# A hybrid decoder layer on one core: the sampled tokens' gate and norm by themselves, values turned through memory, a later residual, another order at the start, the last quarter in parts

## The chip, the cores and the metric

The kernel runs on one core of a Trainium2 chip. A core has TensorE (matrix products and transposes, its results in PSUM), VectorE, ScalarE and GpSimd (elementwise work, sums, activations), SyncE, which here only issues DMA transfers, and DMA engines between device memory and SBUF, the on-chip memory of 128 partitions. Each engine works through its own queue in order and waits on semaphores. The metric is the device time in microseconds, the median of several runs; one further run is profiled.

## The reference

One layer of a decoder for two groups: one new sequence of 1024 tokens ("prompt") and eight sequences with one token each and a carried state ("sample"). Model width 1024, all arrays float32.

```python
proj = rmsnorm(x, norm1_w) @ w_in            # 1024 -> q, f, i, g (1024 each), z (1024), xBC (1536), dt (16)
# group A, HGRN2: 8 heads of 128
f = lb + (1 - lb) * sigmoid(f_r); k = 1 - f; q = silu(q_r); v = i_r
S = f * S + k v^T;  o_a = rmsnorm(q S) * silu(g_r)          # a scan over the tokens
# group B, Mamba-2: 16 heads of 64, 2 groups, state 128
xBC = silu(conv4(xBC)); dt = softplus(dt_r + bias)
S = exp(A dt) S + dt x B^T;  y = S C + D x                  # a scan over the tokens
y = rmsnorm(y * silu(z), per group of 512)
x = x + concat(o_a, y) @ w_out
gate, val = split(rmsnorm(x, norm2_w) @ w_up)               # 2 x 2816
x = x + (silu(conv3(gate)) * val) @ w_down
y = rmsnorm(x, final_norm_w)
```

Both states and the convolutions' last rows are returned too.

## The kernel before, in words

Activations lie with features on partitions and the 1032 tokens (1024 of the prompt, then 8 sampled) along the free axis. Every large product is made of three passes on rounded operands (`fp32r`): high part by high part, low by high, high by low. So each weight tile is loaded (`ws`), rounded on ScalarE (`wh`, L190) and subtracted on VectorE (`wl`, L192); `wload` (from L180) does this with two buffers.

TensorE's order is written by hand. A list of jobs, one for each block of 128 output features of the input projection (three chunks of 344 tokens, 72 matmuls) or two blocks of the output projection, is the main stream. Side streams (the two SSD groups, the eight HGRN heads) are Python generators, and `drive` advances the main stream by a number of matmuls for each weight that a generator yields. `after(n, work)` calls a piece of work n main matmuls later; `spread` does so piece by piece. The other engines' queues are ordered by the framework's scheduler, which follows the order of the program only loosely; `fetch` (L172) keeps a load behind the weight load issued last.

The stages in order of time:

- Start: `first_norm` (L106) norms three tiles of tokens a chunk: squares and root on ScalarE, reciprocal and scaling on VectorE (`xn`, L118), transposes (`tp`), rounding into `hh` and `hl` (L125, L126). Two projection blocks (x8, x10) are interleaved. Their two weight tiles are loaded and rounded before the norms in the program.
- Jobs x0 to x3; then x9, x11, x4 to x7 beside SSD group 0; z0 to z3, f0, q0, v0 beside SSD group 1; sg0 and z4 to z7 alone. `ssm_decode(g, i)` (L625) is the SSD step of the eight sampled tokens for one block: loads of B, C and state, scaling on ScalarE, products on VectorE (L639, L640), GpSimd (L642) and a reduction (L643). It is called as x5, x7, z0, z1 and z4 to z7 begin, and its result goes into the last 8 columns of the block `Xg[g][i]`. `ssm_gate(g)` multiplies all 1032 columns by silu(z) (L671), sums the squares, and `rstd` makes the norm with a product by `ones` (`ms`) and `rstd_of` (L646 to 651). `tail` (L690) scales the four blocks (L694) and stores them to `mix_d`.
- Heads 0 to 7: `head(h)` (from L829) runs beside the jobs f, q, v, sg of head h+1, the last one beside o8.0 to o12.2. It begins with the transposes of `v`: one of the sampled tokens' (`vd`, L834) and eight of 128 by 128 (`vtp`, L839), which ScalarE copies to `vt` (L840). `vt` is first read by `kv` (L958) and then by `o`. Then come seven levels of a tree of products (`a`), with scalings on VectorE (L872, L873), and the storage of `v` is overwritten from the first of them (L901).
- Output projection: rows 8 to 15 of `mix_d` (jobs o8.m, o12.m, each two blocks of features), then rows 0 to 7 in two halves of tokens. `residual_load` and `residual` add the layer's input: `token_blocks` (L770) rearranges it in device memory by 32-token blocks (`xb_d`), VectorE transposes 32 by 32 blocks (L793), and GpSimd adds (L790). This is done in the o8 jobs, whose sums ScalarE copies from PSUM (L1064); the o12 jobs add on VectorE (L1066). The sampled tokens' input is transposed by TensorE for each block (`xtd`, L797), into a PSUM bank of which there is one (`nx`).
- The MLP's up projection (`ua`, `ub`), the down projection (`dn`), whose last four row blocks run quarter by quarter of the tokens in the order 3, 0, 1, 2. After each quarter 128 tokens at a time are transposed back (`fin`, L1461), squared (L1463), rooted, scaled and stored.

Of the kernel before, what the change touches and what calls it, by code (L numbers as in the profile page):

```python
# [16 lines left out]
P = 128  # L17
DM = 1024
# [32 lines left out]
def hybrid_layer(  # L51
# [54 lines left out]
    def first_norm(tiles):  # L106
        xs = []
        for i in tiles:
            xt, t0, n = xtm[i]
            xn = [half("xn"), half("xn")]  # L110
            ss = keep.tile([P, 4], F32, tag="ss", bufs=4, name=nm("ss"))
# [3 lines left out]
            A.activation(ss[:n, 3:4], ss[:n, 2:3], AF.Sqrt, bias=epsc[:n], scale=1.0 / DM)  # L115
            V.reciprocal(ss[:n, 3:4], ss[:n, 3:4])
            for i in range(2):
                V.tensor_scalar(xn[i][:n], xt[:n, i * 512:(i + 1) * 512], ss[:n, 3:4], None, op0=ALU.mult)  # L118
            xs.append((xn, t0, n))
        c0, c1 = xs[0][1], xs[-1][1] + xs[-1][2]  # L120
        for k in range(KT):
            tp = bank("tp")
            for xn, t0, n in xs:
                PE.transpose(tp[:, t0 - c0:t0 - c0 + n], xn[k // 4][:n, (k % 4) * P:(k % 4 + 1) * P], ident[:n, :n])
            A.activation(hT_hi[k][:, c0:c1], tp[:, :c1 - c0], AF.Copy, scale=col("n1", k))  # L125
            V.scalar_tensor_tensor(hT_lo[k][:, c0:c1], tp[:, :c1 - c0], col("n1", k),  # L126
                                   hT_hi[k][:, c0:c1].bitcast(F32), op0=ALU.mult, op1=ALU.subtract)
# [52 lines left out]
    def wload(src, kt, m=P, kept=None):  # L180
# [9 lines left out]
        A.copy(wh[:, :n], ws[:, :n])  # L190
        if not again:
            V.tensor_tensor(wl[:, :n], ws[:, :n], wh[:, :n].bitcast(F32), op=ALU.subtract)  # L192
        if kept is not None:
            if again:
                SP.dma_start(wl.bitcast(F32), wl_d[kept[0]])
            else:
                SP.dma_start(wl_d[kept[0]], wl.bitcast(F32))
# [164 lines left out]

    def xbc_close(j, ext):
# [6 lines left out]
        A.activation(acc[:, T:NT], acc[:, T + 3:T + 32:4], AF.Silu)  # L370
        return acc

    def xbc_job(j, put):
        ext = []
        def begin():
            ext.append(xbc_open())
            if j in (5, 7):
                ssm_decode(0, (5, 7).index(j))
# [13 lines left out]
    first = [(j, wload(w_in_[0, :, OFF_X + j * P:OFF_X + (j + 1) * P], KT), xbc_open()) for j in (8, 10)]  # L392
    for i in range(3, 9):
        load_x(i)
    vec_cols(0)
    for c in range(NCH):
        first_norm(range(3 * c, 3 * c + 3))
# [28 lines left out]
    G.memset(dtr[:, :NT], 0.0)  # L426
# [98 lines left out]
    for g in range(4):  # L525
        rows = slice(32 * g, 32 * g + 32)
        V.tensor_copy(mlow[rows], lowf[rows, :, rows])
        V.tensor_copy(eyec[rows], ident[rows, rows])
# [96 lines left out]
    def ssm_decode(g, i):  # L625
        j = g * 4 + i
        xdd = small.tile([P, 2, ND], F32, tag="xdd", name=nm("xdd"))
        xdec = Xg[g][i][:, T:NT]
# [15 lines left out]
        V.scalar_tensor_tensor(xdec, xdec, d_bc[:, j:j + 1], xdd[:, 1, :], op0=ALU.mult, op1=ALU.add)  # L644

# [7 lines left out]
    def ssm_gate(g):  # L653
        acc = []

        def z_job(i):
            j = g * 4 + i

            def begin():
                if i == 0:  # L660
                    acc.append(tl("g", "gacc"))
                if g:
                    ssm_decode(1, i)
                elif i < 2:
                    ssm_decode(0, i + 2)

            def evict(c, cs, ps):
                Y = Xg[g][i][:, cs]
                sz = tl("z", "sz")[:, :CH]
                A.activation(sz, ps, AF.Silu)  # L670
                V.tensor_tensor(Y, Y, sz, op=ALU.mult)  # L671
# [5 lines left out]
                if i == 3:  # L677
                    after(36 + 14 * g, lambda: rstd(c))
            in_job(f"z{j}", OFF_Z + j * P, evict, begin=begin)

        def rstd(c):
            cs = chunks[c]
            ps = bank("ms", "nx")
            mm(ps[:, :CH], ones, acc[0][:, cs])
            rstd_of(acc[0][:, cs], tl("z", "nt")[:, :CH], ps[:, :CH], 512)
# [4 lines left out]
        def tail():  # L690
            for i in range(4):
                j = g * 4 + i
                Y = Xg[g][i][:, :NT]
                V.scalar_tensor_tensor(Y, Y, col("sn", j), acc[0][:, :NT], op0=ALU.mult, op1=ALU.mult)  # L694
                SP.dma_start(mix_d[8 + j], Y)

# [54 lines left out]
    vd_d = dram.tile([H, ND, P], F32, name="vd_d")  # L751
    hr_d = dram.tile([H, 4, 256], F32, name="hr_d")

    am = const.tile([P, NC, P], F32, name="am")
    G.memset(am, 0.0)
# [3 lines left out]
    V.tensor_tensor(selod, ident[:, 0:ND], ident[:, 32:32 + ND], op=ALU.add)  # L759
# [9 lines left out]

# [736 lines left out]
```

## Time and profile before

| What | us |
|---|---|
| Median of 3 runs | 1764.88 (1764.72 to 1768.95) |
| The profiled execution's own time | 1763.89 |
| Its span, first to last instruction | 1762.2 |
| TensorE busy in it | 1713.2 (97%) |
| VectorE busy | 1105.4 (63%) |
| ScalarE busy | 812.3 (46%) |
| GpSimd busy | 482.0 (27%) |

A row of a group of instructions has line, engine, operation, output and inputs, shape and count, then busy us, mean ns of one, and the engine's idle time just before them with what ended it. A row of a timeline has start and length in us. A row of waits has engine, operation and line, what it waited for, then the sum in us, the times, and the longest. Matmuls overlap one another, so that the time from one's start to the next one's start is shorter than the length that is shown.

### The profile page before, as it was taken

The page shows a single profiled execution, that of the slowest core. Times are in us where ns is not written, and L with a number is a line of the kernel's source. Part 1 is how long each engine was busy: PE and PEld are TensorE (multiplying, and loading weights), DVE is VectorE, ACT ScalarE, POOL GpSimd, SP SyncE. Part 2 cuts the span into 40 slices and gives each one's busy share as a digit, 9 for nine tenths or more (in the row PEclk, how much of TensorE's full clock was granted, in tenths as well). Part 3 has the DMA queues.
Part 4 walks back from the last instruction along what each step waited for, and adds up shares of the span by engine and source line. Part 5 has one row for each costly group of instructions (what it writes and reads, how often), then busy time and mean ns, then how long its engine had stood idle before and what let it go on. Part 6 is the DMA issues. An engine that isn't in the chain of part 4 may idle for free. (4 is left out here: it accounts for less than half of the span.)

```text
span 1762.2 us, 38558 instructions
## 1 busy us (share of the span) xinstructions
PE 1713.2 (97%) x16111; PEld 1662.8 (94%) x16111; DVE 1105.4 (63%) x1988; ACT 812.3 (46%) x1450; POOL 482.0 (27%) x485
## 2 busy tenths in 40 slices
PE   7999899999999999999899999999999999999998
PEld 6999799998999999999799989999999999999997
DVE  6668966575554554466636688776667777445545
ACT  7577698454544454454423374334333434111114
POOL 2103332120110110112220355666666664000002
PEclk9999999999999999999899999999999999999999
DMA  5355744643321332234336742222222226422312
GB/s 166 68 147 155 189 117 136 179 139 105 88 89 51 98 87 80 69 115 143 110 113 212 245 127 73 73 85 85 85 73 73 80 78 217 152 85 78 98 61 97
DMA packets 249828, 199.17 MB, mean 113 GB/s; under 512 B 47212, under 2 KB 220822, under 8 KB 249638
## 3 DMA queue, kind: packets, MB, share of 16 engines
q1 hardware_dynamic: 249366, 196.61, 36.8%
q8 instruction: 126, 2.06, 0.5%
q14 instruction: 48, 0.39, 0.1%
q0 software_dynamic: 288, 0.10, 0.0%
HBM read 154.11 MB, written 46.94 MB: 114 GB/s over the span
## 5 line engine op out<-in xcount | busy, mean ns | idle before, releaser
L93 PE MATMUL mm<-hh,wh 128*128 128x344 f32 x1248 | 405.9, 326 | 2.0 <-issue 1.2
L93 PE MATMUL mm<-hl,wh 128*128 128x344 f32 x1248 | 405.5, 325 | 0.0
L93 PE MATMUL mm<-hh,wl 128*128 128x344 f32 x1248 | 402.4, 323 | 0.0
L93 PEld LDWEIGHTS mm<-hh,wh 128*128 128x128 f32 x1248 | 235.4, 189 | 6.5 <-issue 3.9
L93 PEld LDWEIGHTS mm<-hl,wh 128*128 128x128 f32 x1248 | 235.4, 189 | 4.5 <-issue 3.3
L93 PEld LDWEIGHTS mm<-hh,wl 128*128 128x128 f32 x1248 | 235.7, 189 | 1.8 <-issue 1.4
L190 ACT CAST wh<-ws 128x1024 fp32r<-128x1024 f32 x96 | 100.6, 1047 | 254.1 <-PE dn L93 135.0
L93 PE MATMUL ub<-uh,wh 128*128 128x258 f32 x704 | 199.3, 283 | 3.1 <-DVE fext L1319 2.7
L93 PE MATMUL ub<-ul,wh 128*128 128x258 f32 x704 | 199.0, 283 | 0.0
L93 PE MATMUL ub<-uh,wl 128*128 128x258 f32 x704 | 198.7, 282 | 0.0
L93 PE MATMUL dn<-ah,wh 128*128 128x256 f32 (+1 forms) x640 | 181.1, 283 | 2.0 <-DVE x L1436 2.0
L93 PE MATMUL dn<-al,wh 128*128 128x256 f32 (+1 forms) x640 | 180.6, 282 | 0.0
L93 PE MATMUL dn<-ah,wl 128*128 128x256 f32 (+1 forms) x640 | 180.1, 281 | 0.0
L192 DVE TENSOR_TENSOR wl<-ws,wh 128x1024 fp32r<-128x1024 f32 x88 | 108.7, 1235 | 75.7 <-ACT wh L190 68.6
L93 PE MATMUL mm<-mh,wh 128*128 128x258 f32 x512 | 148.2, 289 | 4.1 <-ACT x L1064 2.8
L93 PE MATMUL ua<-uh,wh 128*128 128x258 f32 x528 | 149.6, 283 | 1.3 <-DVE val L1331 1.3
L93 PE MATMUL ua<-ul,wh 128*128 128x258 f32 x528 | 149.3, 283 | 0.0
L93 PE MATMUL ua<-uh,wl 128*128 128x258 f32 x528 | 148.4, 281 | 0.0
L93 PE MATMUL mm<-ml,wh 128*128 128x258 f32 x512 | 146.9, 287 | 0.8 <-DVE ml L1024 0.8
L93 PE MATMUL mm<-mh,wl 128*128 128x258 f32 x512 | 146.5, 286 | 0.0
L93 PEld LDWEIGHTS ub<-uh,wh 128*128 128x128 f32 x704 | 132.9, 189 | 3.8 <-DVE fext L1319 2.9
L1269 DVE TENSOR_TENSOR wl<-wt,wh 128x512 fp32r<-128x512 f32 x88 | 89.6, 1037 | 74.2 <-ACT wh L1268 73.9
(351 smaller groups left out, 4037.2 us busy)
## 6 DMA issues: line engine op xcount, KB each, us to landing
ws<-in_w_in_dram SPq DMA_DIRECT2D x52, 512.0 KB
ws<-in_w_up_dram SPq DMA_DIRECT2D x44, 512.0 KB
ws<-in_w_out_dram SPq DMA_DIRECT2D x24, 512.0 KB
act_d<-val SPq DMA_DIRECT2D x22, 516.0 KB
al<-act_d SPq DMA_DIRECT2D x22, 516.0 KB
ws<-in_w_down_dram SPq DMA_DIRECT2D x22, 512.0 KB
ml<-mix_d SPq DMA_DIRECT2D x48, 172.0 KB
csb<-cs_d SPq DMA_DIRECT2D x32, 256.0 KB
```

Source lines behind the costliest of these rows:

```text
L93: PE.matmul(out, lhsT, rhs, start=start, stop=stop)
L190: A.copy(wh[:, :n], ws[:, :n])
L192: V.tensor_tensor(wl[:, :n], ws[:, :n], wh[:, :n].bitcast(F32), op=ALU.subtract)
L1269: V.tensor_tensor(lo[:, cs], sums[name], hi[:, cs].bitcast(F32), op=ALU.subtract)
```

## The change

Five parts, shown cut to their core.

**Sampled tokens apart.** `ssm_decode` works in a tile of its own (`xdk`) and not in the last columns of `Xg`; silu(z) of these tokens is kept in `szd`; `decode_gate` and `decode_norm` gate, norm and store them. The prompt's gate, norm and store then cover 1024 columns. `ssm_decode` is called in other jobs: (0,0) in z3, (0,1) to (0,3) in f0, q0, v0, (1,0) in sg0, (1,1) to (1,3) in z4 to z6. The norm of group 1 is called 100 main matmuls after its chunk instead of 50.

```diff
+    def decode_gate(g):
+        V.tensor_tensor(xdk[:, js, :], xdk[:, js, :], szd[:, js, :], op=ALU.mult)
+        V.tensor_tensor(dg[:, 0:4, :], xdk[:, js, :], xdk[:, js, :], op=ALU.mult)
+        V.tensor_reduce(dg[:, 4, :], dg[:, 0:4, :].rearrange("p j b -> p b j"), axis=mybir.AxisListType.X, op=ALU.add)
+        after(40, lambda: decode_norm(g, js, dg))
+
+    def decode_norm(g, js, dg):
+        ps = bank("dgs", "nx")
+        mm(ps[:, :ND], ones, dg[:, 4, :])
+        rstd_of(dg[:, 4, :], dg[:, 5, :], ps[:, :ND], 512)
+        for j in range(js.start, js.stop):
+            V.scalar_tensor_tensor(xdk[:, j, :], xdk[:, j, :], col("sn", j), dg[:, 4, :], op0=ALU.mult, op1=ALU.mult)
+        SP.dma_start(mix_d[8 + js.start:8 + js.stop, :, T:NT].rearrange("j p b -> p j b"), xdk[:, js, :])
...
-                if g:
-                    ssm_decode(1, i)
-                elif i < 2:
-                    ssm_decode(0, i + 2)
+                if g and i < 3:
+                    ssm_decode(1, i + 1)
+                elif j == 3:
+                    ssm_decode(0, 0)
...
+                if c == NCH - 1:
+                    G.tensor_copy(szd[:, j, :], sz[:, n:])
...
-                    after(36 + 14 * g, lambda: rstd(c))
+                    after(36 + 64 * g, lambda: rstd(c))
```

**Values by memory** for heads 0 to 6: the v job stores `v` to `vb_d` in pieces of 32 floats, with the 32 by 32 blocks in their transposed places; the head loads it 60 main matmuls after it began, and VectorE transposes inside the blocks.

```diff
+        def v_end():
+            for b in range(4):
+                SP.dma_start(vb_d[h, :, :, 32 * b:32 * b + 32].rearrange("(a j) c r -> j c a r", j=32),
+                             t["v"][32 * b:32 * b + 32, :T].rearrange("j (c a r) -> j c a r", a=4, r=32))
...
         for hf in range(2):
+            if h < H - 1:
+                later_vt.append((vt[hf], vb_d[h, :, 4 * hf:4 * hf + 4, :]))
+                continue
...
+        def fetch_values():
+            for dst, src in later_vt:
+                fetch(dst.rearrange("p (c n) -> p c n", n=P), src)
+
+        after(60, fetch_values)
...
         V.tensor_copy(odr, ops[:, :P])
+        if h < H - 1:
+            for hf in range(2):
+                V.transpose(vt[hf], vt[hf])
         yield 3.5
```

**Later residual.** Input blocks 0 to 7 are added in o8.4, o8.6, o12.4, o12.6 (two each) instead of o8.0, o8.2, o8.4, o8.6. The sampled tokens' input is loaded once and transposed in one batch into `xsT` by `token_blocks`; GpSimd adds it. `token_blocks` issues a piece every 30 main matmuls instead of 40.

```diff
-            return w, [residual_load(m + i) for i in range(2)] if r0 == 8 else None
+            rm = {(8, 4): 0, (8, 6): 2, (12, 4): 4, (12, 6): 6}.get((r0, m))
+            return w, [(rm + i, residual_load(rm + i)) for i in range(2)] if rm is not None else []
...
-                ps = bank("xtd", "nx")
-                PE.transpose(ps[:, :ND], xd, ident[:ND, :ND])
-                V.tensor_tensor(out[1][:, 508:516], out[1][:, 508:516], ps[:, :ND], op=ALU.add)
+                add(out[1][:, 508:516], xsT[:, m, :])
```

**The start.** The rounding of the first two weight tiles (`hold`) is placed behind the first chunk's norm: the first tile's after the norm's last scaling, the second's after the first rounded activations. Some constants (`eyec`, `selod`, the memsets of `dtr` and `am`) are placed behind the norm too.

```diff
+    def first_rounded():
+        with tc.issue_after(early[0].ins), tc.issue_after(early[1].ins):
+            held[0]()
+        behind.append(early[0].ins)
...
-        first_norm(range(3 * c, 3 * c + 3))
+        first_norm(range(3 * c, 3 * c + 3), *((None, None) if c else (first_rounded, held[1])))
...
-    G.memset(am, 0.0)
+    late(G.memset(am, 0.0))
```

**The last quarter.** Feature blocks 0 to 3 are transposed and squared after the sixth of its eight products, blocks 4 to 6 after the last product, block 7 by itself; the first tile's first half is scaled by ScalarE and GpSimd, the rest by VectorE. The other quarters are as before.

```diff
+            if c == last and m == 5:
+                for t0, n in parts_:
+                    open_.append(opened(t0, n))
+                    turned(open_[-1], 0, range(4), open_[-1][2][0])
+        if c == last:
+            ends = [psmm.tile([P, 512], F32, tag="mm", name=nm("fin7")) for _ in open_]
+            for o in open_:
+                turned(o, 1, range(4, 7), o[2][1])
+            for o, e in zip(open_, ends):
+                turned(o, 2, range(7, 8), e, 3)
+            for q, (o, e) in enumerate(zip(open_, ends)):
+                root(o, True)
+                scaled(o, 0, o[2][0], slice(0, 512), q == 0)
+                scaled(o, 1, o[2][1], slice(0, 384))
+                scaled(o, 1, e, slice(384, 512))
+            for q, i in ((0, 1), (1, 0), (0, 0), (1, 1)):
+                out(open_[q], i)
```

185 lines of the change are left out of this document (123 added, 62 removed).

## The prediction

> **What bounds the kernel now.** I read the busy table first (TensorE 97% of the span), then cut the span into stages, since a mean over stages with different limits says little. The columns: stretch, its length, busy time of TensorE, weight loads, VectorE, ScalarE and GpSimd, granted clock, DMA share, rate.
>
> ```profile
> span 1762.2 us, 38558 instructions
> 0.00:15.00 15.00, 3.59 (x14) 2.44 (x14) 8.25 (x22) 8.69 (x20) 9.01 (x26) 1.00 0.93 310
> 176.00:210.00 34.00, 28.92 (x196) 24.68 (x195) 32.63 (x51) 22.58 (x52) 11.88 (x11) 0.95 0.74 193
> 210.00:384.00 174.00, 171.55 (x1155) 162.11 (x1154) 113.79 (x205) 117.15 (x230) 40.07 (x31) 1.00 0.51 147
> 384.00:412.00 28.00, 24.72 (x507) 23.23 (x507) 25.52 (x39) 18.61 (x24) 5.04 (x4) 0.98 0.47 153
> 412.00:820.00 408.00, 406.80 (x5211) 391.37 (x5210) 209.47 (x404) 191.97 (x309) 33.00 (x24) 1.00 0.29 85
> 820.00:870.00 50.00, 40.19 (x682) 38.12 (x680) 37.66 (x63) 22.13 (x51) 18.82 (x16) 0.90 0.49 147
> 870.00:922.00 52.00, 52.00 (x433) 50.84 (x433) 20.54 (x45) 13.48 (x26) 9.85 (x12) 1.00 0.29 92
> 922.00:1060.00 138.00, 133.59 (x1093) 131.72 (x1092) 97.93 (x176) 67.13 (x118) 45.56 (x45) 1.00 0.60 192
> 1754.00:1763.00 9.00, 0.58 (x6) 0.34 (x4) 3.37 (x8) 2.21 (x8) 0.00 (x0) 0.80 0.34 126
> ```
>
> TensorE sets the end nearly everywhere. It stands idle 11.4 us at the start, 5.1 us in the last part of the first SSD group (176 to 210), 3.3 us where head 0 begins (384 to 412), 9.8 us around head 7 (820 to 870), 4.4 us before the MLP and some 8.4 us at the very end. In the first two of the middle stages VectorE is busy 96% and 91% of the time: it is the bound there, for a while. In the six heads between, TensorE idles 1.2 us in 408. So an instruction taken off TensorE counts in full there, and VectorE work counts in the narrow stages. The waits of TensorE (total us, times, longest) name who ends them:
>
> ```profile
> PE tp L124 <- DVE xn L118: 5.1, 3, 2.5
> PE yo L93 <- DVE S L580: 3.1, 1, 3.1
> PE a L93 <- DVE q L873: 2.8, 1, 2.8
> PE mm L93 <- ACT x L1064: 2.8, 1, 2.8
> PE xtd L797 <- DVE odr L943: 2.6, 1, 2.6
> PE odp L93 <- DVE x L798: 1.5, 1, 1.5
> PE ms L93 <- DVE vd L842: 1.4, 1, 1.4
> ```
>
> **Values by memory (7 of 8 heads).** TensorE loses eight transposes a head. Their place in its timeline (start, length):
>
> ```profile
> 819.30 1.04 PE L839 MATMUL vtp<-ident,v 128*128 128x128 f32 x8
> 820.09 0.37 PE L93 MATMUL mm<-mh,wh 128*128 128x258 f32 x1
> ```
>
> The next matmul starts 0.79 us after the first of them, so 7 x 0.79 = 5.5 us go, in a stage without idle time. Put in their place: four stores a head (28 in all, 128-byte pieces, as the 32 `xb_d` transfers have), two loads, and two VectorE transposes for two ScalarE copies.
>
> ```profile
> L793 DVE STREAM_TRANSPOSE xs<-xs x16: 660/702/714, 783.1 to 913.8; 128x512 f32<-128x512 f32 x16
> L962 DVE COPY SS<-kv 128x128 f32<-128x128 f32 x7 | 2.0, 292 | 29.2 <-PE kv L93 29.2
> L774 SPq DMA_DIRECT2D xb_d<-in_x_prompt_dram x32: 542/668/2742, 30.1 to 219.3; - x32
> DVE xs L793 <- DMA xs<-xb_d: 17.3, 6, 8.6
> SPq L175 <- PE od L93: 65.0, 7, 12.5
> q1 hardware_dynamic: 249366, 196.61, 36.8%
> ```
>
> A VectorE transpose of this shape takes 0.70 us whatever runs beside it, so 1.4 us a head. They stand behind `odr`, ahead of `SS`, where VectorE now idles 29.2/7 = 4.2 us a head. If that cover were gone it would be 9.8 us in all. The stores cost SyncE 4 x 0.67 = 2.7 us a head; they are issued when `v` is evicted, one job before anything overwrites `v`. The mean DMA packet takes 0.368 x 16 x 1762.2 / 249366 = 42 ns, so 7 x 4096 pieces cost at most 28672 x 0.042 / 16 = 75 us of each DMA engine, in a stage whose DMA is busy 29% of 408 us: 47% then, still not the bound. The load is issued at the 60th main matmul of a head and wanted at the 144th ((2.5 + 3 x 4.5)/32 of 4 x 72); 84 of these last at least 84 x 171.55/1155 = 12.5 us (the mean matmul of 210 to 384), against 17.3/6 = 2.9 us that `xs` is typically waited for. I take 1 us for the odd late landing (bounds 0 and 7: one us a head).
>
> The Trainium skill (DMA: Bandwidth & Descriptors, Specifications) speaks against such stores: under 512 B a transfer does not run at line rate, since the engine reads, changes and writes back. By it I would double the price, an estimate: 150 us of each engine, 37 points on top of the 29%, still under the limit and in nobody's way unless a landing is late. No row here separates the 128-byte packets' time.
>
> **Start.** The end of the first norm waits behind other work:
>
> ```profile
> 10.13 1.05 ACT L190 CAST wh<-ws 128x1024 fp32r<-128x1024 f32 x1 [0.38 <-DMA ws<-in_w_in_dram]
> 10.78 0.34 DVE L528 COPY eyec<-ident 32x32 f32<-32x32 f32 x2
> 11.98 1.22 DVE L192 TENSOR_TENSOR wl<-ws,wh 128x1024 fp32r<-128x1024 f32 x1
> 13.12 0.15 DVE L116 RECIPROCAL ss<-ss 128x1 f32<-128x1 f32 x1
> 15.00 0.94 PE L93 MATMUL mm<-hh,wh 128*128 128x344 f32 x2
> ```
>
> The third tile's root stands behind the cast (1.05), its reciprocal behind the constants and `wl` (1.22). With weight rounding and constants later, the reciprocal comes near 11.1, not 13.12. But the same cast and subtraction then stand ahead of the first rounded activations, so I keep 1.7 of the 2.0 us (bounds 0 and 3).
>
> **Sampled tokens.** The decode steps leave the x5, x7, z0, z1 and z7 jobs for z3, f0, q0, v0, sg0. In 176 to 210 VectorE spends on them:
>
> ```profile
> L640 DVE TENSOR_TENSOR Sd<-Sd,Bb 128x512 f32<-128x512 f32 x3 | 3.0, 997 | 0.0
> L643 DVE TENSOR_REDUCE xdd<-Cb 128x4 f32<-128x512 f32 x4 | 2.7, 676 | 1.2 <-POOL Cb L642 1.2
> L639 DVE TENSOR_TENSOR Bb<-Bb,xdd 128x512 f32<-128x512 f32 x2 | 1.8, 916 | 0.0
> ```
>
> 7.5 us of 32.6. Without them VectorE has 25 us of work in a stage that TensorE fills with 29, so the 5.1 us of idle time should mostly go: -4 (bounds 0 and -5). They land in 210 to 384, where VectorE is at 65%. The own gate and norm of the eight tokens add about ten VectorE instructions and a table change a group, all small: +0.5 (0 to 2). The group-1 norm comes 50 main matmuls later (36 + 64 against 50), after head 0 has taken its first products; in its place, head 0's later levels meet this block:
>
> ```profile
> L694 DVE SCALAR_TENSOR_TENSOR xbc<-xbc,vcol,gacc 128x1032 f32<-128x1032 f32 x4 | 4.9, 1289 | 0.0
> ```
>
> The wait of `ms` for `vd` (1.4) goes, the wait of `a` for `q` (2.8) goes or moves one level on: -2 (bounds -3.3 and +2).
>
> **Later residual.** Its loads, transposes and adds leave o8.0 and o8.2, which run beside head 7, for o8.4 to o12.6, which run alone; the eight `xtd` transposes become one batch. Gone with them: the `xtd` wait (2.6), `odp` behind a VectorE that waited 8.6 us for `xs` (1.5), most of the `mm` wait for ScalarE (2.8), and GpSimd adds that slow VectorE. Head 7 keeps its own transposes and the splitting of `ml`. Of 9.8 us idle I count 7 (bounds 3 and 9.8), and 0.5 for `xtd`. In o12.4 and o12.6 (922 to 946) VectorE now also evicts:
>
> ```profile
> L1066 DVE TENSOR_TENSOR x<-x,mm 128x258 f32<-128x258 f32 x16 | 6.7, 420 | 6.4 <-PE mm L93 6.4
> L790 POOL TENSOR_TENSOR x<-x,xs 128x512 f32<-128x512 f32 (+2 forms) x12 | 11.7, 992 | 44.5 <-ACT x L1064 44.5
> ```
>
> Eight transposes (5.6 us) join it, each behind a load, with evictions queued behind them for which TensorE waits: +1.5 (0 to 5).
>
> **Last quarter.** After the last product two tiles go one after the other through squares, root and scaling:
>
> ```profile
> 1753.31 0.60 ACT L1463 ACTIVATE ot<-fin 128x512 f32<-128x512 f32 x1 [2.04 <-PE fin L1461]
> 1755.62 1.41 DVE L1473 SCALAR_TENSOR_TENSOR ot<-fin,fss,fw 128x512 f32<-128x512 f32 x2
> 1757.71 1.41 DVE L1473 SCALAR_TENSOR_TENSOR ot<-fin,fss,fw 128x512 f32<-128x512 f32 x2
> ```
>
> Half the squares move ahead of the end (2 x 0.60), and ScalarE with GpSimd take one scaling of 0.70 from VectorE. Against it stand four short squares with their read-outs, and the shared half passes through two engines: -0.9 (bounds +0.5 and -1.5).
>
> **Sum.** -5.5 + 1 - 1.7 - 4 + 0.5 - 2 - 7 - 0.5 + 1.5 - 0.9 = -18.6 us. The profiled execution took 1763.89 (1.7 around its span), so 1745.3; the median of the runs, 1764.88, lies 1.0 above it: 1746. All best bounds give -5.5 - 3 - 5 - 3.3 - 9.8 - 0.5 - 1.5 = -28.6 (1736), all worst -5.5 + 7 + 2 + 2 - 3 - 0.5 + 5 + 0.5 = +7.5 (1772).
>
> **Rivals.** *The waits move on.* VectorE's work is moved, not removed, and the next stage could stop in its turn. For it: a block of 4.9 us stays in head 0, and o12.4 gets evictions and transposes on one queue. Against it: 65% and 51% VectorE load in the stages that receive. Then only TensorE's own instructions, start and end count, and half of head 7: -5.5 - 0.5 - 1.7 - 0.9 - 3.5 + 4.5 (costs of 1 + 0.5 + 3) = -7.6, so 1757.
>
> *Everything goes well*: no new waits, all named idle time gone: about -26, 1739.
>
> *The values come late* (the slow side). SyncE works in order, and it already waits 65.0/7 = 9.3 us a head for `od` with the next head's state load. If the new load stands behind that wait, it is issued only when VectorE already has the transposes at its front; what is queued behind them, rounding of weights and the state chain, holds TensorE. At the longest `xs` wait, 8.6 us, less the 4.2 us that VectorE has spare, each head loses 4.4: 7 x 4.4 = 31, so 1777. It decides from (18.6 + 5.3)/7 = 3.4 us a head. Against it: 12.5 us between load and use.
>
> By the page's rule of the small transfers this last case would be the likelier, but the 47% and the 12.5 us speak against it.
>
> **Chances.** Forecast 0.62, everything well 0.12, waits move on 0.17, values late 0.09. A measurement here can tell about 0.3% (5.3 us) from no change, so faster means under 1759.6. The first two are faster; of the third two thirds, the rest is within 0.3%; the fourth is slower in 0.06 and within in 0.03. Faster 0.85, same 0.09, slower 0.06. The range 1738 to 1760 leaves out the worst of the third case, most of the fourth and the best of the second, less than 2 in 10.
>
> **What would show it.** No `vtp` but head 7's; heads 1 to 6 about 0.8 us shorter each, with TensorE still idle under 3 us over them; the first product near 13 us; under 2 us idle in the last x jobs; head 7's stage under 4 us idle, with no `xtd` wait; the last 9 us about one shorter. Wrong would be: VectorE waits on the loads of `vt` of several us a head, waits of `mm` for VectorE in o12.4 and o12.6 over 5 us, or a wait of `a` in head 0 as long as before.

## The result and the profile after

The changed kernel took 1767.82 us (median of 20 runs, 1765.51 to 1774.35), the kernel before 1765.11 on the same chips (20 runs, 1761.58 to 1770.98): a ratio of 1.0012 with a 95% interval of 1.0005 to 1.0019. 18.6 us were to be gained; none were. TensorE's own work did become less, 1706.9 us of a span of 1766.2 against 1713.2 of 1762.2, so its idle time rose from 49.0 to 59.3 us.

The stages show where. This is the view of busy time by stretches of the changed kernel, with the columns of the prediction (TensorE, weight loads, VectorE, ScalarE, GpSimd, granted clock, DMA share, rate):

```profile
0.00:15.00 15.00, 5.80 (x25) 4.80 (x26) 7.48 (x21) 10.47 (x26) 9.23 (x26) 1.00 0.93 307
176.00:210.00 34.00, 34.00 (x243) 31.13 (x242) 26.19 (x44) 21.89 (x43) 6.15 (x5) 1.00 0.38 101
210.00:384.00 174.00, 168.16 (x1128) 158.35 (x1126) 128.78 (x236) 119.31 (x250) 53.27 (x45) 1.00 0.65 181
384.00:412.00 28.00, 21.96 (x476) 19.91 (x475) 19.29 (x28) 11.55 (x16) 5.37 (x4) 0.88 0.35 107
412.00:820.00 408.00, 396.01 (x5111) 379.51 (x5110) 201.36 (x410) 181.96 (x288) 29.85 (x24) 1.00 0.35 98
820.00:870.00 50.00, 46.07 (x758) 44.05 (x757) 38.27 (x76) 28.93 (x64) 5.63 (x5) 0.97 0.54 166
922.00:1060.00 138.00, 130.50 (x1053) 127.81 (x1052) 98.69 (x172) 63.43 (x110) 54.46 (x59) 0.99 0.60 192
```

TensorE's idle time fell at the start, in the last x jobs (none in 176 to 210, was 5.1 us) and around head 7 (3.9 us in 820 to 870, was 9.8). It rose in 210 to 384 (5.8 us, was 2.5), where head 0 begins (6.0 us in 384 to 412, was 3.3) and in the six heads that had been full (12.0 us in 412 to 820, was 1.2). Fixed stretches of two kernels do not hold quite the same work, so the table below goes by work: the start of a job's first product on TensorE, read from the timeline, minus the start of the same product in the kernel before (e1 and e6 are the experiments e1_pin and e6_pin_residual_old).

| first product of | before, at us | after | e1 | e6 |
|---|---|---|---|---|
| x0 | 58.38 | -3.35 | -2.75 | -2.30 |
| x7 | 187.12 | -3.37 | -2.88 | -2.22 |
| z0 | 211.71 | -9.32 | -8.84 | -8.17 |
| z3 | 253.97 | -9.30 | -8.81 | -8.15 |
| f0 | 269.68 | -5.46 | -2.53 | -2.38 |
| z4 | 334.52 | -2.88 | -0.91 | -1.23 |
| f1 (head 0 begins) | 384.16 | -6.61 | -5.13 | -5.33 |
| v1 | 417.52 | -1.22 | -7.98 | -8.44 |
| o8.0 (head 7 begins) | 820.09 | +7.69 | -11.17 | -12.74 |
| o12.0 | 865.20 | -1.25 | -22.23 | -20.06 |
| o12.6 | 932.16 | -4.40 | -25.38 | -23.31 |
| third job after o12.6 | 955.12 | -0.11 | -21.11 | -22.89 |
| up projection | 1039.11 | +0.39 | -18.17 | -21.86 |
| end of the span | 1762.16 | +4.08 | -14.38 | -18.07 |

A difference that rises from one row to the next is a loss in between. Three stand out: 6.4 us from z3 to z4, which give back what had been won from x7 to z0 (6.0); 14.3 from f1 to o8.0, where 5.5 were to be gained; and 4.3 behind o12.6. Against them stand 8.9 us that head 7's stage gained (o8.0 to o12.0). The waits of TensorE and VectorE in the changed kernel that bear on this (total us, times, longest):

```profile
PE ms L93 <- DVE nt L695: 7.0, 3, 6.0
PE mm L93 <- DVE x L1151: 4.2, 6, 1.1
PE a L93 <- DVE q L954: 3.9, 3, 2.9
PE ms L93 <- DVE gacc L727: 3.6, 1, 3.6
DVE vt L1027 <- DMA vt<-vb_d: 47.8, 12, 6.0
```

VectorE waits 47.8 us for the loads of the values, 12 times, and the tree products `a` and the norm's `ms` wait for VectorE. (The row of `gacc` lies ahead of the heads, between z3 and f0, and is taken up with the sampled tokens' steps.) VectorE's timeline in one head, and that of SyncE's queue beside it (start, length; in brackets the idle time and what ended it):

```profile
707.71 0.69 DVE L954 TENSOR_TENSOR q<-v,tt 128x512 f32<-128x512 f32 x1
712.87 0.71 DVE L1027 STREAM_TRANSPOSE vt<-vt 128x512 f32<-128x512 f32 x1 [4.47 <-DMA vt<-vb_d]
719.63 0.71 DVE L1027 STREAM_TRANSPOSE vt<-vt 128x512 f32<-128x512 f32 x1 [6.05 <-DMA vt<-vb_d]
720.27 0.40 DVE L978 COPY_PREDICATED amc<-mlow,a 128x256 f32<-128x256 uint8 x1
720.58 0.68 DVE L953 TENSOR_TENSOR f<-f,tt 128x512 f32<-128x512 f32 x1
...
735.63 0.28 DVE L1024 COPY odr<-od 128x128 f32<-128x128 f32 x1
```

```profile
706.05 0.43 SPq L182 DMA_DIRECT2D vt<-vb_d  x1
711.77 2.75 SPq L930 DMA_DIRECT2D out_dram<-Sh  x2
714.56 0.51 SPq L182 DMA_DIRECT2D vt<-vb_d  x1
```

The program writes the two transposes behind the copy `odr`. In VectorE's queue they stand 16 and 23 us ahead of it (719.63 and 712.87 against 735.63), in the middle of the tree's levels; when the first of them starts, the second load has not even been issued (714.56). From 708.40 to 720.27 VectorE does nothing but these two transposes: the mask copy (L978) and the scalings (L953, L954) of the next levels stand behind them in its queue, and TensorE waits for these (the longest wait of `a` for `q`, 2.9 us, ends at 722.00, behind the scalings that follow at once).

### The profile page after: what moved, and what is told of

It is laid out like the page before. It is cut to its first block, busy times and chain, and to the rows that moved or that the text cites. A ratio compares the mean times of both kernels' runs of the same rounds, so it can differ in the third digit from the quotient of the medians.

```text
span 1766.2 us, 38579 instructions
## 1 busy us (share of the span) xinstructions
PE 1706.9 (97%) x16059; PEld 1656.1 (94%) x16059; DVE 1101.0 (62%) x2018; ACT 803.7 (46%) x1443; POOL 482.1 (27%) x502
## 2 busy tenths in 40 slices
DMA packets 281925, 206.52 MB, mean 117 GB/s; under 512 B 77564, under 2 KB 251110, under 8 KB 281734
```

## The experiments

Each was measured against the kernel before on the same chip. A ratio is to the kernel before, with its 95% interval. The experiments ran on four chips, on which the kernel before has medians from 1765.2 to 1766.1 us; differences between two medians of the table carry that much beside their own noise.

| Kernel | median us (runs) | ratio |
|---|---|---|
| changed kernel | 1767.82 (20) | 1.0012 (1.0005 to 1.0019) |
| e1_pin | 1749.06 (4) | 0.9905 (0.9891 to 0.9918) |
| e2_tail_old | 1767.68 (11) | 1.0008 (0.9999 to 1.0017) |
| e3_decode_old | 1770.42 (12) | 1.0025 (1.0014 to 1.0035) |
| e4_values_pe | 1760.35 (7) | 0.9975 (0.9963 to 0.9987) |
| e5_pin_tail_old | 1748.62 (5) | 0.9900 (0.9884 to 0.9915) |
| e6_pin_residual_old | 1746.32 (4) | 0.9889 (0.9873 to 0.9905) |
| e7_pin_start_old | 1748.23 (5) | 0.9898 (0.9881 to 0.9915) |
| e8_pin_norm_early | 1754.30 (6) | 0.9934 (0.9920 to 0.9948) |
| e9_norm0_late | 1756.91 (9) | 0.9959 (0.9945 to 0.9972) |
| e10_before_values | 1765.89 (12) | 1.0010 (0.9998 to 1.0022) |
| e11_residual_all_old | 1755.23 (6) | 0.9946 (0.9931 to 0.9961) |
| e12_decode_old | 1748.05 (6) | 0.9905 (0.9889 to 0.9922) |
| e13_before_batch | 1759.32 (6) | 0.9968 (0.9957 to 0.9980) |
| e14_before_values_norm | 1758.49 (6) | 0.9964 (0.9952 to 0.9977) |
| e15_before_three | 1747.88 (4) | 0.9907 (0.9894 to 0.9921) |
| e16_norm_alone | 1758.73 (11) | 0.9972 (0.9961 to 0.9983) |
| e17_batch_norm | 1752.29 (5) | 0.9925 (0.9911 to 0.9938) |

### The order of VectorE's queue

**e1_pin** holds the two transposes back until `odr` has been issued; nothing else changes.

```diff
-        V.tensor_copy(odr, ops[:, :P])
+        odr_ = V.tensor_copy(odr, ops[:, :P])
         if h < H - 1:
-            for hf in range(2):
-                V.transpose(vt[hf], vt[hf])
+            with tc.issue_after(odr_.ins):
+                for hf in range(2):
+                    V.transpose(vt[hf], vt[hf])
```

> The changed kernel, with the two VectorE transposes of vt queued behind the copy of odr, where the program has them. Theory A (they were issued some 16 us earlier than the program places them, and VectorE stood 47.8 us on their loads with the level updates queued behind): the waits of VectorE on the loads of vt fall under 5 us, the heads from f1 to o8.0, which lost 14.3 us against the kernel before, gain 4 to 6 instead, and the span falls by 15 to 20 us to 1746 to 1751. Rival B (the stores and loads themselves slow the heads, by DMA and by SyncE, wherever the transposes stand): the waits move to the place behind odr, kv comes late, and less than 5 us are gained. Rival C (the later norm of group 1 is what stops head 0, 6 us of the 14): the wait of ms stays at 6 us and only 8 to 10 us are gained.

Measured: 1749.06 us, 18.8 under the changed kernel, as theory A has it. VectorE and SyncE in the same head, and the stage of the six heads:

```profile
717.96 0.68 DVE L954 TENSOR_TENSOR q<-q,tt 128x512 f32<-128x512 f32 x1
718.56 0.28 DVE L1024 COPY odr<-od 128x128 f32<-128x128 f32 x1
718.76 1.30 DVE L1028 STREAM_TRANSPOSE vt<-vt 128x512 f32<-128x512 f32 x2
```

```profile
694.69 0.43 SPq L182 DMA_DIRECT2D vt<-vb_d  x1
699.38 2.75 SPq L930 DMA_DIRECT2D out_dram<-Sh  x2
702.17 0.50 SPq L182 DMA_DIRECT2D vt<-vb_d  x1
```

```profile
412.00:820.00 408.00, 404.17 (x5291) 388.15 (x5288) 217.81 (x429) 190.35 (x304) 34.54 (x28) 1.00 0.37 104
820.00:870.00 50.00, 49.41 (x691) 47.83 (x692) 37.12 (x79) 21.23 (x48) 8.70 (x12) 1.00 0.48 149
```

The transposes follow `odr` at once and wait for nothing; no wait of VectorE for `vt` is left among its waits. SyncE issues the second load as late as before, behind the two stores of `Sh` (699.38), and it does not matter: from 702.17 to 718.76 there are 16.6 us. So the loads, the stores and SyncE's late issue are all still there and hold nobody up. The late issue made the second wait of the changed kernel longer (6.05 us), but that anybody waited came from the order of VectorE's queue. The wait of `ms` for `nt` (6.0 us) is gone too: in the changed kernel VectorE had stood in the same way before the transposes at 393.62 (3.27 us) and 396.20 (1.87 us), directly ahead of `nt`.

**e4_values_pe** takes the other way round: all eight heads' values by TensorE, the rest of the change kept.

```diff
-            if h < H - 1:
+            if False:
                 later_vt.append((vt[hf], vb_d[h, :, 4 * hf:4 * hf + 4, :]))
...
-        if h < H - 1:
-            for hf in range(2):
-                V.transpose(vt[hf], vt[hf])
```

> The changed kernel with the values of all heads transposed by TensorE, as in the kernel before; the other four parts stay. Theory A: the heads lose the waits on the loads but pay the eight transposes again (0.87 us a head), so about 20 - 6 = 14 us faster than the changed kernel, some 1752. Rival B says the same; the difference between this run and the one with the pinned transposes is what values by memory are worth when they are not in the way: 6 us by A, 0 or less by B. Rival C: 6 us of wait of ms stay, about 1758.

Measured: 1760.35 us, 7.5 under the changed kernel, 11.3 above e1. None of the three expectations has this right: it is 8 us above the theory's 1752, and the wait of `ms` for `nt`, by which rival C came to 1758, is 0.3 us. Still, the values by memory, as they were ordered, cost the change more than they brought; in their right order they bring something. How much is taken up again below.

### The last quarter and the start

**e2_tail_old** and **e5_pin_tail_old** give the changed kernel and e1 the last quarter of the kernel before (the loop over the quarters as in the diff's removed lines).

> The changed kernel with the last quarter (and the closing of the other quarters) as in the kernel before. From the start of the last four row blocks to the end the change took 42.2 us against 39.6. Theory: the parts cost 2.6 us, since the squares of the last tiles write into buffers whose stores have not landed and eight transposes stand ahead of the last products; undone, 2 to 3 us come back. Rival (the 2.6 us are only a shift of one DMA wait in the sampled tokens' tile, 1.3 us against 0.3, which varies from run to run): under 1 us.

> e1_pin (the transposes of the values placed behind the copy odr), with the last quarter and its closing as in the kernel before. Theory (the closing in parts is worth nothing that can be measured: earlier squares save what the extra read-outs, the eight transposes ahead of the last products and the two-engine half cost): within 1 us of e1_pin, so 1748 to 1750. Rival 1 (it costs what the one profile of the changed kernel suggested from the last down block to the end): 2 to 3 us faster, 1746 to 1747, and the stretch from the start of the last down product to the end is 2 us shorter. Rival 2 (it gains the predicted 0.9): 1750, the last 9 us about 1 us longer.

Measured: 1767.68 beside 1767.82 (the rival), and 1748.62 beside 1749.06 (the theory). The closing in parts is worth nothing that can be measured. The changed kernel's profile had lost 2.6 us from the start of the last four row blocks of the down projection to the end (from +1.49 to +4.08 against the kernel before). The profile of e5, with the old closing, loses 1.7 there too (from -16.92 to -15.24), so most of it does not come from the closing. The kernels below show with what it goes: with the old closing and the values by memory, e10, e14 and e15 lose 1.9, 2.2 and 1.7 us in this stretch; with the values by TensorE, e13, e16 and e17 lose 0.4, 0.0 and 0.4, and e4, with the new closing, 0.6. Why values that were used up long before cost something there was not followed.

**e7_pin_start_old** rounds the first weight tiles ahead of the norm again.

```diff
-    first = [(j, wload(w_in_[0, :, OFF_X + j * P:OFF_X + (j + 1) * P], KT, hold=held), xbc_open()) for j in (8, 10)]
+    first = [(j, wload(w_in_[0, :, OFF_X + j * P:OFF_X + (j + 1) * P], KT), xbc_open()) for j in (8, 10)]
...
-        with tc.issue_after(early[0].ins), tc.issue_after(early[1].ins):
-            held[0]()
...
-        first_norm(range(3 * c, 3 * c + 3), *((None, None) if c else (first_rounded, held[1])))
+        first_norm(range(3 * c, 3 * c + 3), *((None, None) if c else (first_rounded, None)))
```

> e1_pin, with the first two weight tiles rounded as soon as they are there, ahead of the norm, as before (the constants stay behind the norm). Theory (the order of the rounding is the gain of the start, 2.6 to 3.4 us at the first products, and it lasts to the end because TensorE is full behind it): first product near 14.5 us, 1751.5 to 1752.5. Rival 1 (the constants alone made the gain): first product under 13 us and 1749. Rival 2 (the gain is used up in the waits of the jobs x9 to x11): first product near 14.5 us, and 1749 to 1750.

Measured: 1748.23 us. The first product of x8 starts at 14.78 us instead of 12.86, and x0 3.4 us later than in e1, as the theory said. At z4 the difference is 1.2 us, at the end of the span 0.4: the second rival. The gain of the start is there and is used up on the way; one place is job x9, beside which the product `xp` waits 1.5 us for ScalarE's `xbc` in e1 (at 115.33) and not in e7.

### The sampled tokens' steps

**e3_decode_old** (on the changed kernel) and **e12_decode_old** (on e6, below) call the decode steps where the kernel before called them, and group 0's own gate later, since its last step now comes later.

```diff
-                if g and i < 3:
-                    ssm_decode(1, i + 1)
-                elif j == 3:
-                    ssm_decode(0, 0)
+                if g:
+                    ssm_decode(1, i)
+                elif i < 2:
+                    ssm_decode(0, i + 2)
...
-                if h == 0:
-                    i = "fqvs".index(n[0])
-                    ssm_decode(*((0, i + 1) if i < 3 else (1, 0)))
...
             ext.append(xbc_open())
+            if j in (5, 7):
+                ssm_decode(0, (5, 7).index(j))
...
-            after(60, lambda: decode_gate(0))
+            after(280, lambda: decode_gate(0))
```

> The changed kernel with the decode steps called in the jobs of the kernel before (x5, x7, z0, z1, z4 to z7); own tile, own gate and norm stay. The change gained 7.4 us in x6 and x7 and lost 6.4 us from z3 to sg0. Theory D (VectorE's load is what matters, and it has been moved from one narrow stage into another): both go away, and the span changes by -1 to +3 us; x6 to z0 loses 5 to 7 us again, z3 to z4 gains 5 to 6. Rival E (the loss from z3 to sg0 comes from the own gate and norm and the copies for it, not from the place of the steps): the loss stays, and the kernel is 6 to 8 us slower than the changed one. Rival F (the gain in x6 and x7 comes from the earlier start, not from the decode steps): the gain stays and the loss goes, 5 to 6 us faster.

> e6_pin_residual_old with the decode steps called in x5, x7, z0, z1, z4 to z7 as before and group 0's own gate later, so only their place is undone. Theory (the place gains 6 us in the last x jobs and gives 5 of them back where the decode step of z3 holds up the sums of group 0's norm, so that 1 to 3 us remain): 1747.5 to 1749.5, with over 4 us more between x7 and z0 and 4 less between z3 and f0. Rival 1 (the predicted 4 us remain): 1750 or more. Rival 2 (the place is worth nothing): 1745.5 to 1747.

Measured: 1770.42, 2.6 above the changed kernel, and 1748.05, 1.7 above e6, as theory D and the theory of e12 have it; the intervals overlap both times. The two stretches of e12, and of e6 behind them:

```profile
176.00:210.00 34.00, 28.06 (x190) 24.55 (x190) 29.16 (x49) 19.60 (x41) 13.86 (x11) 0.95 0.63 159
210.00:384.00 174.00, 174.00 (x1174) 165.47 (x1173) 119.63 (x222) 122.61 (x237) 46.15 (x39) 1.00 0.54 153
```

```profile
176.00:210.00 34.00, 34.00 (x243) 31.13 (x243) 27.05 (x47) 21.90 (x42) 6.15 (x5) 1.00 0.36 99
210.00:384.00 174.00, 168.83 (x1127) 159.39 (x1126) 129.12 (x237) 120.03 (x252) 52.97 (x45) 0.99 0.66 183
```

Idle time moved: 5.9 us leave the first stretch and 5.2 appear in the second. What stands there, in e6's VectorE timeline and the waits of its TensorE:

```profile
259.77 0.68 DVE L668 TENSOR_TENSOR Sd<-Sd,Bb 128x512 f32<-128x512 f32 x1
261.97 0.69 DVE L671 TENSOR_REDUCE xdd<-Cb 128x4 f32<-128x512 f32 x1 [1.51 <-POOL Cb L670]
262.57 0.51 DVE L727 TENSOR_TENSOR gacc<-gacc,sz 128x344 f32<-128x344 f32 x1
```

```profile
PE ms L93 <- DVE gacc L727: 4.1, 1, 4.1
```

The sum of squares `gacc`, for which the norm's product waits, stands behind a reduction of the decode step that waits for GpSimd.

**e9_norm0_late** tried to remove that wait by calling group 0's norm later, on e6: `after(36 + 64 * g, ...)` becomes `after(100, ...)`.

> e6_pin_residual_old (values pinned behind odr, input added in the o8 jobs) with the norm of group 0 called 100 main matmuls after its chunk, as that of group 1, instead of 36. Theory (the product ms waits 4.1 us there because the sums gacc stand on VectorE behind a reduction of the first decode step, which waits 1.5 us for GpSimd; later nobody waits): the wait of ms for gacc falls under 1 us, f0 starts 4 us earlier, 1742 to 1743. Rival 1 (the wait only moves: another stop of VectorE or ScalarE takes its place by z4): 1745.5 to 1747. Rival 2 (the four scalings and the norm of group 0 then stand in the way of group 1's work): 1748 or more.

Measured: 1756.91, 10.6 slower than e6: the second rival, by more than it said. f0 does start 6.5 us earlier and no wait of `ms` for `gacc` is left, but the later block meets worse neighbours:

```profile
PE mm L93 <- ACT q L886: 6.3, 2, 5.4
...
PE ms L93 <- DVE nt L695: 5.5, 3, 2.9
```

From f0 to sg0, where group 1's scan and the decode steps run, TensorE loses 18.0 us against the kernel before (from -8.87 to +9.09).

### Head 0 and the bank that several products share

**e8_pin_norm_early** is e1 with group 1's norm after 50 main matmuls, as before; **e16_norm_alone** is the kernel before with only that norm after 100 (`36 + 14 * g` against `36 + 64 * g`, the one line).

> e1_pin, with the norm of group 1 called 50 main matmuls after its chunk, as before, instead of 100. Theory (the later call frees head 0's beginning, as the prediction had it, 2 us): 1751, with a wait of the first tree product a for a scaling of q of 2 to 3 us where the heads begin. Rival 1 (with the transposes of the values pinned behind odr, VectorE has room there and the place of the norm does not matter): 1748.5 to 1749.5. Rival 2 (the later call does harm because its four scalings of 1.3 us stand in front of head 0's levels): 1746 to 1748.

> The kernel before with only the norm of group 1 called later. Theory (it removes the waits of ms for vd, 1.4 us, and of a for q, 2.8 us, as the prediction had it): 1762 to 1763.5. Rival 1 (its four scalings hold head 0's levels, and nothing is gained): 1764.5 to 1766. Rival 2 (the gain is larger because the bank nx is free for head 0): 1759 to 1761.

Measured: 1754.30, 5.2 above e1 (the theory had 2); and 1758.73 (the theory had 1762 to 1763.5), which is under the kernel before by 6.5 us by the medians and 4.9 by the ratio (0.0028 x 1765). One number in one line carries about a third of the whole gain. In e16's profile the waits of `ms` for `vd` (1.4) and of `a` for `q` (2.8) are gone, and from z7 to v1 it gains 5.2 us on the kernel before (from +0.57 to -4.59). Another 2.6 come from o8.0 to o12.0, where `xtd` waits 1.3 us instead of 2.6, and 2.0 are lost again before the up projection. So the two waits were worth about what their rows say; the prediction had counted half of them.

**e10_before_values** adds the values by memory, pinned, to the kernel before, alone (the diff of the change for them, with the order of e1).

> The kernel before with one part of the change alone: values by memory for heads 0 to 6, the transposes on VectorE pinned behind odr. Theory (TensorE loses 0.79 us a head and VectorE's and ScalarE's order in the heads gains besides, as the 11.3 us between e1_pin and the kernel with all values by TensorE say): 1754 to 1756, 9 to 11 us under the kernel before. Rival 1 (only TensorE's own transposes go, 7 x 0.79): 1759.5. Rival 2 (without the other parts the loads of the values are late or the gain of the heads is lost around head 7): 1762 or more.

Measured: 1765.89 us, no gain: the second rival. From f1 to o8.0 the heads do become 5.9 us shorter (from +5.19 to -0.72), but head 0 starts 5.2 us late. TensorE, then VectorE, ahead of it:

```profile
382.51 0.27 PE L841 MATMUL vd<-ident,v 128*8 128x128 f32 x1
388.55 1.51 PE L93 MATMUL ms<-gacc,ones 128*128 128x344 f32 x2 [5.77 <-DVE vd L853]
```

```profile
386.11 0.69 DVE L864 TENSOR_TENSOR Sh<-Sh,f 128x512 f32<-128x512 f32 x1 [2.15 <-DMA Sh<-in_state_hgrn_dram]
386.72 0.51 DVE L671 TENSOR_TENSOR xbc<-xbc,sz 128x344 f32<-128x344 f32 x1
387.79 0.52 DVE L676 TENSOR_TENSOR gacc<-gacc,sz 128x344 f32<-128x344 f32 x1 [0.56 <-ACT sz L675]
388.22 0.27 DVE L853 COPY vd<-vd 8x128 f32<-8x128 f32 x1
```

`vd` and `ms` use the one PSUM bank `nx`. TensorE has nothing between the two now, and the small copy that frees the bank (0.27 us) stands on VectorE behind a state product that waits for a load. The later norm takes `ms` out of this place.

**e14_before_values_norm** has both, the values and the later norm.

> The kernel before with the values by memory (pinned) and the norm of group 1 called 100 main matmuls after its chunk instead of 50. Theory (without the eight transposes TensorE comes 5.8 us too early to the product ms, whose bank vd holds until VectorE copies it; the later call frees it, so that the values then show their gain): 1756 to 1760, with waits of ms for vd and of a for q under 1 us each. Rival 1 (the norm's place gains, but the values alone gain nothing beyond it): equal to e16_norm_alone within 1 us. Rival 2 (the decode steps of z4 to z7, which stay where they were, hold VectorE there): 1763 or more.

Measured: 1758.49, the same as the norm alone: the first rival. At o8.0 it is 5.9 us ahead of e16 (-10.65 against -4.76); then the gain goes, 2.3 of it at o12.0, where `xtd` waits 4.4 us instead of 1.3, the rest in single steps later.

### The residual

**e6_pin_residual_old** is e1 with the residual in the o8 jobs (its edit is below); **e11_residual_all_old** is e6 with the sampled tokens' input per block too; **e13_before_batch** is the kernel before with only that input in one batch (the lines for `xtd` and `xsT` of the change).

```diff
-            rm = {(8, 4): 0, (8, 6): 2, (12, 4): 4, (12, 6): 6}.get((r0, m))
+            rm = {(8, 0): 0, (8, 2): 2, (8, 4): 4, (8, 6): 6}.get((r0, m))
```

> e1_pin, with the input blocks added in o8.0, o8.2, o8.4, o8.6 as before (the sampled tokens' input still comes in one batch). Theory (the later residual is worth about 12 us of the stage beside head 7 and costs about 4 in o12.4 and o12.6): 8 us slower, 1757; between 820 and 870 us TensorE idles over 8 us again, and the waits of mm for the adds on VectorE in the o12 jobs (5.7 us in e1_pin) fall under 2. Rival 1 (that stage gained because the values no longer pass ScalarE and TensorE while head 7 runs, so most of it stays): 1748 to 1751. Rival 2 (the waits in o12.4 and o12.6 cost more than the later place brings): 1745 to 1747.

> e6_pin_residual_old with the sampled tokens' input loaded and transposed for each block, as before, instead of in one batch: the whole residual is then that of the kernel before. Theory (what e6_pin_residual_old still gains between o8.2 and o12.0, 6.7 us, is the batch: no wait for the transpose xtd and no product odp behind a VectorE that waits for it): 4 to 7 us slower, 1750 to 1753, with a wait of xtd over 2 us. Rival 1 (it is the values and the sampled tokens' own gate that free that stage; the batch is worth its 0.5 us): 1746 to 1747.5.

> The kernel before with the sampled tokens' input loaded once and transposed in one batch; the place of the residual as before. Theory (each xtd takes the one PSUM bank nx, which od holds until VectorE has copied it to odr; TensorE stands 2.6 us there in the kernel before, 1.5 at odp and 2.8 at mm for ScalarE's copies that come late in consequence; the batch is taken long before): 4 to 8 us faster than before, 1757.5 to 1761.5, no wait of xtd, and 4 to 7 us more busy time of TensorE between 820 and 870 us. Rival (the 8.9 us between e6_pin_residual_old and e11_residual_all_old need the new values or the sampled tokens' own gate): 1764 to 1766.

Measured: e6 1746.32, 2.7 under e1 with intervals that overlap, where the theory had it 8 us above: the second rival. e11 1755.23, 8.9 above e6, more than the theory's 4 to 7; e13 1759.32, 5.9 under the kernel before, as its theory has it. On the whole the later place brings nothing that shows, the batch nearly all. By the table the later place does gain in head 7's stage (11.1 us from o8.0 to o12.0 in e1, 7.3 in e6) and gives as much back behind o12.6 (4.3 lost in e1, 0.4 in e6). TensorE's timeline of e11 beside head 7, and the stage in e6 and in e11:

```profile
842.25 0.22 PE L856 MATMUL xtd<-ident,xd 8*128 8x8 f32 x1 [4.35 <-DVE odr L1021]
...
854.59 0.39 PE L93 MATMUL odp<-selod,odr 128*128 128x8 f32 x2 [1.52 <-DVE x L857]
```

```profile
820.00:870.00 50.00, 45.56 (x536) 43.79 (x534) 38.80 (x70) 21.08 (x46) 15.65 (x16) 0.97 0.46 144
```

```profile
820.00:870.00 50.00, 40.49 (x474) 38.38 (x474) 34.09 (x65) 19.57 (x44) 13.67 (x13) 0.93 0.37 111
```

`xtd`, `od` and `odp` pass the same bank `nx` on: `xtd`, a transpose of 0.22 us, waits 4.35 us until VectorE has copied `od` to `odr`, and `odp` waits for VectorE to add `xtd`. TensorE is idle both times. The batch also saves six of eight small loads and moves the eight small adds from VectorE to GpSimd; what these are worth was not measured apart.

**e15_before_three** is the kernel before with the values (pinned), the later norm and the batch; **e17_batch_norm** the same without the values.

> The kernel before with three edits: values by memory (pinned), the later norm of group 1, the batch of the sampled tokens' input. Theory (the three carry the gain of e6_pin_residual_old, and start, own gate and the decode steps' place carry at most 3 us): 1747 to 1751. Rival (the own gate and norm of the sampled tokens are needed): 1754 or more.

> The kernel before with the batch of the sampled tokens' input and the later norm of group 1, the values still by TensorE; beside e15_before_three it shows what the values are worth when nothing behind them takes their gain. Theory (the values are worth the 5.5 us of TensorE's transposes, 7 x 0.79, as the prediction had it): 1753 to 1754. Rival 1 (they are worth the 11.3 us that e4_values_pe lies above e1_pin): 1758 to 1760. Rival 2 (nothing is left of them, as in e14_before_values_norm against e16_norm_alone): 1747.5 to 1749.5.

Measured: 1747.88, as the theory has it, and 1752.29, 1 us under its theory. Three of the edits make the whole gain of e1 (1749.06) and e6 (1746.32), within the noise. The values' share is 4.4 us by the medians, 3.2 by the ratios (0.0018 x 1765), with intervals that overlap: nearest the theory's 5.5, not to be told more closely. The 11.3 us between e4 and e1 cannot all be the values' own time: e4 lies 4.5 us behind e1 at f1 already, when only head 0's eight transposes have run. What else it loses was not followed.

## Why the prediction was wrong

**Values by memory: the step that failed.** The prediction put the VectorE transposes "behind `odr`, ahead of `SS`". That is their place in the program, and that VectorE's queue would keep it was taken without a reason, though the scheduler follows the program only loosely. In the queue they stood 16 us and more ahead of it, among the levels; VectorE waited there 47.8 us for the loads, 6.8 a head, which the prediction itself names as a sign of being wrong. 1 us was set for late landings, with 7 at worst, where the heads lost 14.3 and 5.5 were to be won. e1, which restores the place and nothing else, took 1749.06. The rest of that working held: the difference to the kernel before falls by 0.9 us at the start of each of the jobs f3 to f7, where the `vtp` transposes had been; a VectorE transpose took 0.71 us; the DMA share in the heads rose to 35% only (47% was allowed for). The slow rival ("the values come late") had the direction, but another mechanism: it set the transposes at VectorE's front because the load would come late behind SyncE's wait for `od`. The wait that stood ahead of the second load was one for `Sh` (its stores start at 711.77, when GpSimd's sum has ended at 711.74); e1 keeps it, and it costs nothing there.

**That e1 comes within 3 us of 1746 is largely luck.** The terms below were off on both sides and cancel: the start and the last quarter brought nothing that shows, the decode steps about 2 us of 4 and the later residual nothing on balance of its 7, while head 0 brought 5 to 6.5 instead of 2 and the batch 6 to 9 instead of 0.5.

**Start, -1.7.** The first product came 2.6 us earlier, more than predicted, and the end did not (e7). A gain at the start counts only if no later wait is bound to something else than TensorE; here about 2 us of it had gone by z4.

**Decode steps, -4.** The 5.1 idle us of the last x jobs went, as written. But "VectorE is at 65%" was read as room in the receiving stage; a mean says nothing of the place. The step landed ahead of `gacc`, behind GpSimd, and 6.3 us were lost from z3 to f0 (e1). Of the forecast, about 2 us remain (1.7 in e12, 2.6 in e3, neither clear of the noise). The +0.5 for the own gate was not measured apart; e15 does without it and is as fast.

**Head 0, -2 (bounds -3.3 and +2).** Mis-sized: 5 to 6.5 us alone (e16), 5.2 within the change (e8). In the changed kernel it was covered by the misplaced transposes.

**Later residual, -7, batch -0.5, evictions +1.5.** The stage was read rightly, its cause not. The `xtd` wait (2.6) and the `odp` wait (1.5) stood in the quoted rows and were put to the residual's place; they belong to the shared bank, and the batch frees it: 5.9 us alone, 8.9 in e6 against e11. The later place has 3.7 us of its own in that stage (e1 against e6), and it pays as much behind it: that the evictions of o12.4 and o12.6 cost something was right, but it was 4.3 us from o12.6 on, in the changed kernel and in e1, against 0.4 in e6, and not 1.5. The two VectorE shares named against the waits moving on (65% and 51%) leave out the stage that takes over these additions: in the prediction's own table VectorE is busy 97.93 of 138 us there, 71%.

**Last quarter, -0.9.** None (e2, e5), within its bounds.

## What to carry to other kernels

The order of a program is not the order of a queue: where a framework's scheduler orders the engines, look in the trace for every operation that waits for a DMA, or tie it to its place: two transposes of 0.71 us that had moved 16 and 23 us ahead held all ready work behind them, and cost 18.8 us. Where a wait stands between two small products, ask whether they share a PSUM bank before costing the work around them: eight transposes of 0.22 us, done early in one batch, were worth 5.9 us, a norm called 50 matmuls later 5 to 6.5. A stall that is removed is worth only what the next stage can use, so the parts of a change are to be measured alone and together: the values were worth 0 on the kernel before, 0 beside the later norm, 3 to 4 us beside the norm and the batch, and up to 11 beside all the other parts.

## What the hardware showed beyond that

The pieces of 128 bytes did no visible harm. The changed kernel and e1 move the same packets, 77564 of them under 512 bytes, and e1 is 18.8 us faster by the order of one queue; in e1 the DMA share of the heads is 37% where the kernel before had 29%. Their price can be read from the packet records of the traces: e1 has 61440 packets of 128 bytes with a mean of 13.3 ns, the kernel before 32768 with a mean of 13.1 ns. The 28672 pieces more are 24 us of each of the 16 DMA engines, where the prediction allowed 75 by the mean packet's 42 ns and 150 doubled. Byte for byte they are dear all the same: a packet of 512 bytes takes 29 ns in both traces. A load of `vt` landed 5.1 to 6.8 us after SyncE began to issue it (714.56 to 719.63, 706.05 to 712.87), longer than the 2.9 us that the prediction took from the waits for `xs`, which are what was left of a load's time when VectorE came to it and not its length.
